# Output projection of a hybrid layer: eight units on features against seven half-size products on tokens

## The chip, the cores and the metric

The kernel runs on one core of one Trainium2 chip. The metric is the device time of one execution in microseconds (us), lower is better. Five engines of the core matter here, each with its own in-order queue: TensorE (PE, with its weight load PEld), VectorE (DVE), ScalarE (ACT), GpSimd (POOL), and SyncE (SP), which only issues transfers. DMAs are issued from the SP, ACT and POOL queues. A queue whose first instruction waits holds everything behind it.

## The reference, cut to what matters

One layer, D = 1024, S = 512 tokens, d_ff = 2816, float32 throughout:

```
u      = RMSNorm(x) * g1
z      = u @ w_in
A, B   = MoBA attention(z), chunkwise mLSTM(z)
merged = sigmoid(z_gA) * (A @ w_proj_a) + sigmoid(z_gB) * (B @ w_proj_b)
h      = x + merged @ w_out              # w_out is 1024 x 1024: the output projection
u      = RMSNorm(h) * g2
g, up  = split(u @ w_gate_up)
h      = h + (silu(g) * up) @ w_down
out    = RMSNorm(h) * g3
```

The change is in the line of `w_out` and in what leads from it into `w_gate_up`.

## The kernel before, in words

**Precision.** A float32 product is computed as three matmuls: an operand is split into a high part (rounded by an ACT copy, L148) and a low part (a DVE subtraction, L161), and high·high, low·high and high·low are accumulated in PSUM (`mm3`, L199 to L203). Every weight block therefore costs one ACT and one DVE instruction beside its matmuls.

**Up to the output projection.** Activations stand with features on the partitions and the 512 tokens along the free axis. `UNITS` lists 60 blocks of weights of 128x1024 in the order of their use: q, k, va, ob, vb, qkb, then `ga` and `gb` (gates, units 28 to 43), `p` (the two branch projections, 44 to 51) and `wo` (52 to 59). SP loads them in that order, 512 KB each, into seven buffers (`load_pair`, L186); `split_unit` makes high and low parts two units ahead. A unit is 24 matmuls of 128x512. `run_p` multiplies the projections by the sigmoid gates (L595 to L597) and splits the merged activations into `mgh` and `mgl`.

**The output projection before.** `run_wo(m)` gives 128 output features for all 512 tokens: 24 matmuls, DVE adds the residual (`xr`, L663), the ACT squares the sum (`add_sq`, with a running sum on DVE, L265), and the block is scaled by the second norm's gain (L669, L670, L678, L679). `residual()` transposes the previous block's sum to tokens (L647, four transposes), and stores it in DRAM as `h1d`, to which the down projection later adds.

**The feed-forward part.** Each of 22 `gu` items is a gate-and-up block computed as seven products of half size instead of eight (a Winograd form of Strassen's scheme): the activations are four quarters (two halves of the features by the two halves `A_` and `B_` of the tokens) and their sums, the seven operands `bq` being numbered 0 to 6; the weights are W11, W12, W22 and the sums S1 to S4, each product 12 matmuls of 128x256. `gu_load` loads the weights; the sum of two blocks (`s13`) is formed on the way in, by a POOL transfer that adds to what it finds (L705). S2 and S4 are formed by two DVE additions (L751, L752). The down projection (`ds`) uses the same scheme on tokens and adds its results to `h1d` by POOL transfers (L921).

**What sets the order.** A scheduler takes instructions by a priority. For the feed-forward part `plan()` gives each product a nominal start, and `at(key, w, off)` sets the priority of what follows to that start plus an offset. The queues keep that order at run time whatever the real times are. In the mLSTM, four loads of `R` from DRAM (L1377) stand on POOL's queue; L1389 is the first DVE instruction to use each.

Of the kernel before, what the change touches and what calls it, by code (L numbers as in the profile page):

```python
# [15 lines left out]
P = 128  # L16
# [31 lines left out]
WO = (0, 4, 1, 5, 2, 6, 3, 7)  # L48
# [36 lines left out]
def hybrid_layer_kernel(ctx: ExitStack, tc, xT, wall, wgu, wds, wdl, g3v, vecs, wgates, consts, rope, out):  # L85
# [103 lines left out]
    def split_unit():  # L189
# [3 lines left out]
        if u % 2 == 1:  # L193
            load_pair() if u < NGEN - 4 else st["load"]()

    def mm3(ps, wh, wl, wk, rh, rl, start, stop):

        n = len(wk)
        for j, k in enumerate(wk):  # L199
# [3 lines left out]
            T.matmul(ps, wh[:, c], rl[j], start=False, stop=stop and j == n - 1)  # L203
# [184 lines left out]
    def proj(wh, wl):  # L388
        ps = mmb()
        mm3(ps, wh, wl, range(8), uh, ul, True, True)  # L390
# [194 lines left out]
    def run_p(m, wh, wl):  # L585
        if m >= 6:
            load_xr()
        pa, pb = mmb(), mmb()
        mm3(pa, wh, wl, range(4), [t[0] for t in ya], [t[1] for t in ya], True, True)
        mm3(pb, wh, wl, range(4, 8), [t[0] for t in yb], [t[1] for t in yb], True, True)  # L590
# [6 lines left out]
        V.tensor_tensor(ga, ga, gb, op=ALU.add)  # L597
        mgd.append(split_hl(ga, "mg"))
# [4 lines left out]
    xr = []  # L603
    h1d = dram.tile([4, P, D], F32, name="h1d")
    ng2 = cst.tile([P, KT], F32, name="ng2")

    def load_xr():
        m = WO[len(xr)]
        t = act.tile([P, S], F32, name=nm("xr"), tag="X", bufs=NX)
        nc.sync.dma_start(t, xT[m])  # L610
        xr.append(t)

    bq = {}
    ut = {}  # L620
    HS = S // 2

    def bop(o, k):

        if o < 6:
            t = bq[(o // 2, k // 2)].rearrange("p x c -> p (x c)")
            b = 1024 * (k % 2) + HS * (o % 2)
            return t[:, b : b + HS], t[:, b + 512 : b + 512 + HS]
        t = bq[(3, 0)][:, k, :]
        return t[:, 0:HS], t[:, HS:S]  # L630

    def bpair(q, k):
# [6 lines left out]
    trq = []

    def residual():

        while trq:
            m, h = trq.pop(0)
            ps = sb()
            for t in range(4):
                T.transpose(ps[:, t * P : (t + 1) * P], h[:, t * P : (t + 1) * P], ident)  # L647
            o = slot(name="ht")
            act_(o, ps, AF.Copy)
            nc.scalar.dma_start(  # L650
                h1d[:, :, m * P : (m + 1) * P].rearrange("t p c -> p t c"), o.rearrange("p (t c) -> p t c", t=4)
            )

    def run_wo(i, wh, wl):
        if len(xr) < KT:
            load_xr()
        ps = mmb()
        mm3(ps, wh, wl, range(8), [t[0] for t in mgd], [t[1] for t in mgd], True, True)
        residual()
        yield  # L660
        m = i
        h = xr[WO.index(m)]
        V.tensor_tensor(h, ps, h, op=ALU.add)  # L663
        trq.append((m, h))
        a, b = h[:, 0:HS], h[:, HS:S]
        g, ng = col(G2 + m), ng2[:, m : m + 1]
        if m < 4:
            u = ut[m] = slot(name="ut")
            V.tensor_scalar(u[:, 0:HS], a, g, None, op0=ALU.mult)  # L669
            V.scalar_tensor_tensor(u[:, HS:S], b, ng, u[:, 0:HS], op0=ALU.mult, op1=ALU.add)  # L670
            hh, ll = bpair(0, m)
            act_(hh, u, AF.Copy, scale=-1.0)
            V.scalar_tensor_tensor(ll, u, -1.0, f(hh), op0=ALU.mult, op1=ALU.subtract)
        else:
            k = m - 4
            u = ut.pop(k)
            v = slot(name="v1")
            V.tensor_scalar(v[:, 0:HS], a, g, None, op0=ALU.mult)  # L678
            V.tensor_scalar(v[:, HS:S], b, ng, None, op0=ALU.mult)  # L679
            split_hl(v, dst=bpair(1, k))  # L680
            w = slot(name="v2")
            V.tensor_tensor(w[:, 0:HS], u[:, HS:S], v[:, HS:S], op=ALU.subtract)
            V.tensor_tensor(w[:, HS:S], u[:, 0:HS], w[:, 0:HS], op=ALU.subtract)
            split_hl(w, dst=bpair(2, k))
            V.tensor_tensor(u[:, 0:HS], v[:, 0:HS], w[:, 0:HS], op=ALU.subtract)
            if k == 0:
                bq[(3, 0)] = slot4(F32R, "bq")
            split_hl(u[:, 0:HS], dst=bop(6, k))
        add_sq(2, h, WO.index(m))

    run["wo"] = run_wo


# [5 lines left out]

    def gu_load(i):  # L700
# [3 lines left out]
        nc.sync.dma_start(s13, wgu[i][:, None, 0:512].to_broadcast([P, 2, 512]))  # L704
        nc.gpsimd.dma_start(s13, wgu[i][:, 512:1536].rearrange("p (x c) -> p x c", x=2), accum_op=ALU.add)  # L705
# [8 lines left out]
    def plan():  # L714
# [19 lines left out]
    def gu_prep(i):  # L734
        key = ("gu", i)
        g = sw[key]
        r, s13, w11 = g["r"], g["s13"], g["w11"]

        def hl(w, src, dst):
            at(key, w, -H_OFF)  # L740
            act_(dst[0], src, AF.Copy)
            at(key, w, -L_OFF)
# [46 lines left out]
    def prod(ps, w, o, first=False):  # L789

        wh, wl = w
        for k in range(4):
# [4 lines left out]
            T.matmul(ps, wh[:, c], bl, start=False, stop=k == 3, skip_group_check=not first)  # L797

    A_, B_ = slice(0, HS), slice(HS, S)

    def gu_first(i):
# [4 lines left out]
        prod(g["X"], g["W11"], 0, first=True)  # L806
# [4 lines left out]
    def gu_main(i):  # L811

        key = ("gu", i)
        g = sw[key]
        x, s12 = g["X"], g["s"]
        at(key, "S2")
        prod(x, g["S2"], 4)
        at(key, "S2", R_OFF)
        act_(s12[:, B_], x, AF.Copy)
# [9 lines left out]
        if i == 0:
            residual()  # L830
            rb2 = st["rb2"] = rstd_rows([ssum[2]])

            rc, nrc = st["rc"], st["nrc"] = [cst.tile([P, 4], F32, name=n_) for n_ in ("rc2", "nrc2")]
            columns(rb2[0:1, :], rc.rearrange("p (j h) -> p j h", h=1))
# [808 lines left out]
```

## Time and the profile before

| | |
|---|---|
| median of 3 runs | 733.4 us (733.3 to 733.64) |
| span of the profiled execution, first to last instruction | 731.3 us |
| PE busy | 721.8 us (99%) |
| DVE busy | 619.3 us (85%) |
| ACT busy | 431.4 us (59%) |
| POOL busy | 65.6 us (9%) |
| chain of work that ended last | PE 98% |
| granted TensorE clock, mean | 0.998 |

The page gives the profiled execution no time of its own beside the span; the span is 2.1 us below the median of the runs. Busy time of PE is modelled from matmul starts, and consecutive matmuls overlap in the rows, so the time that one takes on the path is the distance between the starts, not its duration. Times inside the trace are counted from the span's start. The output projection runs from about 349 to 399 us.

### The profile page before, as it was taken

The page shows a single profiled execution, that of the slowest core. Times are in us where ns is not written, and L with a number is a line of the kernel's source. Part 1 is how long each engine was busy: PE and PEld are TensorE (multiplying, and loading weights), DVE is VectorE, ACT ScalarE, POOL GpSimd, SP SyncE. Part 2 cuts the span into 40 slices and gives each one's busy share as a digit, 9 for nine tenths or more (in the row PEclk, how much of TensorE's full clock was granted, in tenths as well). Part 3 has the DMA queues.
Part 4 walks back from the last instruction along what each step waited for, and adds up shares of the span by engine and source line. Part 5 has one row for each costly group of instructions (what it writes and reads, how often), then busy time and mean ns, then how long its engine had stood idle before and what let it go on. Part 6 is the DMA issues. An engine that isn't in the chain of part 4 may idle for free.

```text
span 731.3 us, 11389 instructions
## 1 busy us (share of the span) xinstructions
PE 721.8 (99%) x4191; PEld 636.5 (87%) x4191; DVE 619.3 (85%) x1104; ACT 431.4 (59%) x747; POOL 65.6 (9%) x88
## 2 busy tenths in 40 slices
PE   9999999999999999999999999999999999999995
PEld 6888888888888888888888998999899899899984
DVE  6898877899987669566788999899899899989996
ACT  7535776668846339523456656665655565655555
POOL 0004010000000000000000000400310310130000
PEclk9999999999999999999999999999999999999999
DMA  8778573232431222534767353975995795596403
GB/s 315 273 226 226 185 215 110 80 125 94 164 136 58 87 86 88 173 106 124 185 177 203 128 160 93 240 216 128 210 266 146 167 276 166 146 249 200 151 0 117
DMA packets 51320, 118.74 MB, mean 162 GB/s; under 512 B 5292, under 2 KB 10292, under 8 KB 51264
## 3 DMA queue, kind: packets, MB, share of 16 engines
q1 hardware_dynamic: 37024, 88.95, 35.9%
q0 software_dynamic: 9728, 26.80, 19.2%
q10 hardware_dynamic: 4512, 2.26, 1.1%
q8 instruction: 33, 0.54, 0.3%
q14 instruction: 23, 0.19, 0.1%
HBM read 101.17 MB, written 16.82 MB: 161 GB/s over the span
## 4 chain that ended last, share of the span: by engine, by line
PE 98%; DMA 0%; ACT 0%; issue 0%; DVE 0%; SPq 0%; ACTq 0%
PE mm L201 13%; PE mm L203 12%; PE mm L202 12%; PE mm L795 6%; PE mm L796 6%; PE mm L797 6%; PE s L795 3%; PE s L797 3%; PE s L796 3%; PE mm L904 3%; PE mm L905 2%; PE mm L906 2%; PE mm L291 2%; PE acc L1358 2%; PE mm L479 2%; PE mm L480 2%
## 5 line engine op out<-in xcount | busy, mean ns | idle before, releaser
L148 ACT ACTIVATE wh<-raw 128x1024 fp32r<-128x1024 f32 x58 | 61.2, 1058 | 78.7 <-PE mm L202 75.7
L161 DVE TENSOR_TENSOR wl<-raw,wh 128x1024 fp32r<-128x1024 f32 x58 | 70.4, 1219 | 7.3 <-ACT wh L148 6.4
L795 PE MATMUL mm<-bq,w 128*128 128x256 f32 x264 | 75.5, 286 | 0.0
L796 PE MATMUL mm<-bq,w 128*128 128x256 f32 x264 | 74.9, 284 | 0.0
L797 PE MATMUL mm<-bq,w 128*128 128x256 f32 x264 | 74.8, 283 | 0.0
L743 DVE TENSOR_TENSOR w<-s,w 128x1024 fp32r<-128x1024 f32 x44 | 53.6, 1218 | 8.3 <-ACT w L148 8.1
L148 ACT ACTIVATE w<-s 128x1024 fp32r<-128x1024 f32 x44 | 46.5, 1056 | 14.5 <-PE mm L202 5.4
L201 PE MATMUL mm<-u,wh 128*128 128x512 f32 x136 | 53.6, 394 | 0.0
L202 PE MATMUL mm<-u,wl 128*128 128x512 f32 x136 | 53.2, 391 | 0.0
L203 PE MATMUL mm<-u,wh 128*128 128x512 f32 x136 | 53.1, 390 | 0.0
L203 PE MATMUL mm<-ul,wh 128*128 128x512 f32 x136 | 52.9, 389 | 0.0
L202 PE MATMUL mm<-uh,wl 128*128 128x512 f32 x136 | 52.9, 389 | 0.0
L201 PE MATMUL mm<-uh,wh 128*128 128x512 f32 x136 | 52.9, 389 | 0.0
L705 POOL DMA_DIRECT2D s<-in_wgu_dram x22 | 19.0, 862 | 368.0 <-DVE ga L597 132.0
L795 PEld LDWEIGHTS mm<-bq,w 128*128 128x128 f32 x264 | 50.6, 192 | 0.7 <-ACT s L148 0.3
L796 PEld LDWEIGHTS mm<-bq,w 128*128 128x128 f32 x264 | 50.6, 192 | 0.3 <-issue 0.2
L797 PEld LDWEIGHTS mm<-bq,w 128*128 128x128 f32 x264 | 50.6, 192 | 0.1
L148 ACT ACTIVATE w<-raw 128x1024 fp32r<-128x1024 f32 (+2 forms) x44 | 43.7, 995 | 11.7 <-PE s L796 3.3
L797 PE MATMUL s<-bq,w 128*128 128x256 f32 x176 | 49.8, 283 | 0.0
L796 PE MATMUL s<-bq,w 128*128 128x256 f32 x176 | 49.8, 283 | 0.0
L795 PE MATMUL s<-bq,w 128*128 128x256 f32 x176 | 49.8, 284 | 0.0
L148 ACT ACTIVATE w<-sw 128x1024 fp32r<-128x1024 f32 x20 | 21.2, 1060 | 22.4 <-DVE sw L782 20.3
(399 smaller groups left out, 2219.0 us busy)
## 6 DMA issues: line engine op xcount, KB each, us to landing
raw<-in_wall_dram SPq DMA_DIRECT2D x58, 512.0 KB, 3.6
s<-in_wgu_dram SPq DMA_DIRECT2D x22, 512.0 KB, 4.7
s<-in_wgu_dram POOLq DMA_DIRECT2D x22, 512.0 KB, 5.9
raw<-in_wgu_dram SPq DMA_DIRECT2D x22, 512.0 KB, 4.9
raw<-in_wds_dram SPq DMA_DIRECT2D x20, 512.0 KB, 5.9
w<-in_wgu_dram SPq DMA_DIRECT2D x22, 256.0 KB, 6.4
h1d<-s POOLq DMA_DIRECT2D x16, 256.0 KB, 8.8
R<-scr POOLq DMA_DIRECT2D x4, 896.0 KB, 4.6
```

The lines of the kernel that those rows point to most:

```text
L148: return A.activation(out_, in_, func, **kw)
L161: V.tensor_tensor(l, src, f(h), op=ALU.subtract)
L201: T.matmul(ps, wh[:, c], rh[j], start=start and j == 0, stop=False)
L202: T.matmul(ps, wl[:, c], rh[j], start=False, stop=False)
L203: T.matmul(ps, wh[:, c], rl[j], start=False, stop=stop and j == n - 1)
L291: T.matmul(ps01[j], w[:, j * P : (j + 1) * P], r, start=k == 0 and n == 0, stop=k == KT - 1 and n == 2)
L705: nc.gpsimd.dma_start(s13, wgu[i][:, 512:1536].rearrange("p (x c) -> p x c", x=2), accum_op=ALU.add)
L743: V.tensor_tensor(dst[1], src, f(dst[0]), op=ALU.subtract)
L795: T.matmul(ps, wh[:, c], bh, start=first and k == 0, stop=False, skip_group_check=not first)
L796: T.matmul(ps, wl[:, c], bh, start=False, stop=False, skip_group_check=not first)
L797: T.matmul(ps, wh[:, c], bl, start=False, stop=k == 3, skip_group_check=not first)
L904: T.matmul(ps, bh, wh[:, d], start=first and k == 0, stop=False, skip_group_check=not first)
```

## The change

**What it does.** The eight `wo` units are replaced by the seven-product scheme, with the four quarters of the merged activations (feature halves by token halves) as the stationary operand and the blocks of `w_out`, 512 columns wide, as the moving one: seven products (W11, W12, S1, S2, S4, S3, W22) of two token tiles of 12 matmuls each. The results stand on tokens.

- *Activations.* `run_p` writes the merged block into `mT`; `quarters_lo`, `quarters_a` and `quarters_b` form the seven operands `mq` with DVE sums and a high and a low part each.
- *Weights' sums.* S1, S2, S3 and S4 of `w_out` (`ws`), the sums `s13` of the first three `gu` items (`gs`) and S2, S4 of item 2 (`gt24`) are formed in DRAM: a copy on SP's queue (`wo_copy`), then an adding transfer on POOL's queue (`wo_sum`), placed by `SUMS` behind units 18 to 41 in issue order only (`behind` adds an order between instructions, no wait on the chip).
- *Residual.* Result tiles `ht[t, j]` are 128 tokens by 512 features. For the four tiles that a product writes first, ACT copies the PSUM bank and a POOL transfer adds `x` to the copy (L961); for the other four SP loads `x` (L973). All further products are added or subtracted by DVE (L965).
- *Back to features.* `to_features` (L935) transposes each tile, 32 transposes in all; ACT squares tiles with a summed output, stores them to `h1d`, and evicts the transposed blocks with the gain. `norm2` makes the norm from the four columns of sums on 128x4 tiles, and spreads it with one `ones` matmul in place of `rstd_rows` and its way through DRAM.
- *Order.* A table `Q` of offsets sets the priorities. The first products of `gu` items 0 and 1 are interleaved.

The diff, cut to its core:

```diff
-    u += [("wo", m) for m in WO]
+SUMS = {
+    18: [(1, "S1", (1, 0))], 20: [(0, "S1", (1, 1))], 22: [(1, "S2", "S1"), (1, "S3", (0, 0))],
+    24: [(0, "S2", (0, 0))], 27: [(1, "S4", "S2")], 29: [(0, "S4", (0, 1))], 31: [(0, "S3", (1, 0))],
+    33: [(1, 0, None), (1, 1, None)], 35: [(0, 0, None)], 36: [(0, 1, None), (1, 2, None)], 37: [(0, 2, None)],
+    38: [(1, i, "g") for i in G24], 39: [(0, i, "g") for i in G24], 41: [(0, i, "w") for i in G24],
+}
...
+            if u in SUMS:
+                with behind("unit"):
+                    for job, k, src in SUMS[u]:
+                        (wo_copy if job else wo_sum)(k, src)
...
-        mgd.append(split_hl(ga, "mg"))
+        V.tensor_tensor(mT[m // 4][:, m % 4, :], ga, gb, op=ALU.add)
+        if m == 3:
+            quarters_lo(mq, mT[0], slice(0, 4))
...
+    def wo_copy(k, src):
...
+        for e in range(2):
+            nc.sync.dma_start(ws[k][e], ws[src][e] if src in ws else wwo[src][e])
+
+    def wo_sum(k, src):
...
+        for e in range(2):
+            nc.gpsimd.dma_start(ws[k][e], wwo[src][e], accum_op=ALU.add, max_dma_last_dim=1024)
...
     def gu_load(i):
...
-        nc.sync.dma_start(s13, wgu[i][:, None, 0:512].to_broadcast([P, 2, 512]))
-        nc.gpsimd.dma_start(s13, wgu[i][:, 512:1536].rearrange("p (x c) -> p x c", x=2), accum_op=ALU.add)
+        if i < NGS:
+            nc.sync.dma_start(s13, gs[i])
...
+    def wo_prod(ps, w, o, t, first=False):
+        c = slice(t * P, (t + 1) * P)
+        for k in range(4):
+            h, l = w[k]
+            bh, bl = (x[:, 0, c] for x in bview(mq, o, slice(k, k + 1)))
+            T.matmul(ps, bh, h, start=first and k == 0, stop=False, skip_group_check=not first)
+            T.matmul(ps, bh, l, start=False, stop=False, skip_group_check=not first)
+            i = T.matmul(ps, bl, h, start=False, stop=k == 3, skip_group_check=not first)
...
+                marks[k, t] = wo_prod(bank[t], w[k], o, t, first=first)
+                at(WO_ITEM, k, U * (t + 1) + Q["add" + k])
+                if (t_ + t, j) not in ht:
+                    h = ht[t_ + t, j] = slot(name="ht")
+                    i = act_(h, bank[t], AF.Copy, scale=1.0 if op == ALU.add else -1.0)
+                    at(WO_ITEM, k, U * (t + 1) + Q["x"])
+                    marks["x"] = raw_ins(
+                        nc.gpsimd.dma_start(h, xtm[t_ + t][:, j * S : (j + 1) * S], accum_op=ALU.add)
+                    )
+                else:
+                    h = ht[t_ + t, j]
+                    i = V.tensor_tensor(h, h, bank[t], op=op)
...
+        stage("W11", 0, X, 0, 0, ALU.subtract, first=True)
...
+        stage("W12", 2, Y, 0, 0, ALU.add, first=True)
...
+        to_features("S1", Q["t00"], 0, 0)
+        stage("S1", 1, Z, 2, 1, ALU.add, first=True)
...
+        stage("S2", 4, X, 2, 0, ALU.subtract)
...
+        stage("S4", 3, Z, 2, 0, ALU.subtract)
+        to_features("S3", Q["t10"], 1, 0)
...
+        stage("S3", 5, X, 2, 1, ALU.add)
...
+        last_ = stage("W22", 6, X, 0, 1, ALU.add)
```

**PE, the start of the output projection.** Before, a unit's weight block (`wh`, `wl`) is the stationary operand and the merged activations (`mgh`, `mgl`) the moving one, and 24 matmuls into one bank `mm` stand between two groups of transposes; the rows are the end of the second unit.

```order
L201 MATMUL mm_3455<-mgh_3356,wh_3360 128x512
L202 MATMUL mm_3455<-mgh_3356,wl_3361 128x512
L203 MATMUL mm_3455<-mgl_3357,wh_3360 128x512
L201 MATMUL mm_3455<-mgh_3401,wh_3360 128x512
L202 MATMUL mm_3455<-mgh_3401,wl_3361 128x512
L203 MATMUL mm_3455<-mgl_3402,wh_3360 128x512
L647 MATMUL s_3480<-con,xr_3323 128x128 x4
```

After, on the same engine, 12 matmuls of the same size form one token tile of a product (the bank is `mm` or `acc`, the stationary quarter `bq`, the moving weights `w`); these rows are the end of the product W11 and the start of W12.

```order
L916 MATMUL mm_3492<-w_3347,bq_3253 128x512
L914 MATMUL mm_3492<-w_3347,bq_3253 128x512
L915 MATMUL mm_3492<-w_3348,bq_3253 128x512
L916 MATMUL mm_3492<-w_3347,bq_3253 128x512
L914 MATMUL acc_3518<-w_3351,bq_3457 128x512
L915 MATMUL acc_3518<-w_3352,bq_3457 128x512
L916 MATMUL acc_3518<-w_3351,bq_3457 128x512
```

The 192 matmuls of eight units became 168 of seven products, all of 128x512.

**DVE, around the first use of a tile with `x` added.** Before, DVE at the projection's first blocks reads PSUM and `xr` that SP loaded long ago (L663).

```order
L663 TENSOR_TENSOR xr_3323<-mm_3411,xr_3323 128x512
L669 TENSOR_SCALAR ut_3437<-xr_3323,vec 128x256
L161 TENSOR_TENSOR wl_3557<-raw_3366,wh_3556 128x1024
L670 SCALAR_TENSOR_TENSOR ut_3437<-xr_3323,ng_274,ut_3437 128x256
L673 SCALAR_TENSOR_TENSOR bq_3440<-ut_3437,bq_3440 128x512
L663 TENSOR_TENSOR xr_3368<-mm_3455,xr_3368 128x512
```

After, the first row below adds the product W12 to `ht_3489`, the tile that ACT wrote and POOL's transfer added `x` to; behind it in DVE's queue stand low parts of operands (L648) and of weights (L764).

```order
L965 TENSOR_TENSOR ht_3489<-ht_3489,acc_3518 128x512
L648 TENSOR_TENSOR bq_3468<-mT_3112,bq_3468 128x1024
L764 TENSOR_TENSOR w_3547<-raw_3508,w_3546 128x1024
L965 TENSOR_TENSOR ht_3505<-ht_3505,acc_3532 128x512
L764 TENSOR_TENSOR w_3551<-raw_3510,w_3550 128x1024
L648 TENSOR_TENSOR bq_3472<-mT_3112,bq_3472 128x1024
L764 TENSOR_TENSOR w_3617<-raw_3554,w_3616 128x1024
L764 TENSOR_TENSOR w_3621<-raw_3556,w_3620 128x1024
L764 TENSOR_TENSOR w_3695<-raw_3624,w_3694 128x1024
L965 TENSOR_TENSOR ht_3558<-ht_3558,mm_3476 128x512
```

A DVE instruction that needs a transfer's landing now stands ahead of nine others; nine rows behind the last one shown stands the addition of S4's product to the same `ht_3558`, which PE's transposes at the start of S3 read.

**POOL, from the loads of `R` to the output projection.** Before, the four loads of `R` are followed by the additions to the `gu` items' weights (`s`).

```order
L1377 DMA R_1764<-scr 128x1792
L1377 DMA R_2047<-scr 128x1792
L1377 DMA R_2124<-scr 128x1792
L1377 DMA R_2287<-scr 128x1792
L705 DMA s_3562<-in_wgu_dram 128x1024
L705 DMA s_3674<-in_wgu_dram 128x1024
```

After, sums of the weights in DRAM (`ws`, 512 KB each) stand before and between them, and the additions of `x` (`ht`) follow.

```order
L728 DMA ws_276<-in_wwo_dram 512x256
L728 DMA ws_277<-in_wwo_dram 512x256
L1662 DMA R_2145<-scr 128x1792
L728 DMA ws_278<-in_wwo_dram 512x256
L728 DMA ws_279<-in_wwo_dram 512x256
L1662 DMA R_2310<-scr 128x1792
L728 DMA ws_280<-in_wwo_dram 512x256
L728 DMA ws_281<-in_wwo_dram 512x256
```

The last load of `R` moved behind six adding transfers, the nearest two (`ws_278`, `ws_279`, the sum S4) directly ahead of it.

More of the change, by code (lines that the diff above doesn't have):

```diff
@@ L202, in mm3 @@
             T.matmul(ps, wl[:, c], rh[j], start=False, stop=False)
-            T.matmul(ps, wh[:, c], rl[j], start=False, stop=stop and j == n - 1)
+            i = T.matmul(ps, wh[:, c], rl[j], start=False, stop=stop and j == n - 1)
+        return raw_ins(i)
     man = ExitStack()
@@ L389, in proj @@
         ps = mmb()
-        mm3(ps, wh, wl, range(8), uh, ul, True, True)
+        marks["unit"] = mm3(ps, wh, wl, range(8), uh, ul, True, True)
         return ps
@@ L639, in hybrid_layer_kernel @@
[L639 to L659, printed above, removed]
-        yield
[L661 to L689, printed above, removed]
@@ L691, in hybrid_layer_kernel, with bview @@
-    run["wo"] = run_wo
+    ht = {}
+    mT = []
+    mq, bq = {}, {}
+    def bview(ops, o, k):
+        if o not in ops:
+            ops[o] = slot4(F32R, "bq")
+        t = ops[o].rearrange("p a c -> p (a c)")
+        n = HS * (k.stop - k.start)
+        return [t[:, 1024 * e + HS * k.start : 1024 * e + HS * k.stop].rearrange("p (k c) -> p k c", c=HS) for e in range(2)]
+    def bop(o, k):
+        t = bq[o].rearrange("p a c -> p (a c)")
+        return t[:, HS * k : HS * k + HS], t[:, 1024 + HS * k : 1024 + HS * k + HS]
@@ new lines, in hybrid_layer_kernel, with behind @@
+    marks = {}
+    @contextmanager
+    def behind(*keys):
+        traced = nc.cur_bb.bb.instructions
+        last = traced[-1]
+        yield
+        start = next(k for k in reversed(range(len(traced))) if traced[k] is last) + 1
+        for i in traced[start:]:
+            for key in keys:
+                m = marks[key]
+                tc.add_manual_dep(
+                    i, m.name,
+                    mybir.DependencyInfo(mybir.DependencyClass.NoSync, mybir.DependencyReason.DATA),
+                    reason="behind",
+                )
@@ L700, in gu_load @@
+    gs = [dram.tile([P, 2, S], F32, name=nm("gs")) for _ in range(NGS)]
     def gu_load(i):
@@ L796, in prod @@
             T.matmul(ps, wl[:, c], bh, start=False, stop=False, skip_group_check=not first)
[L797 to L799 removed]
+            i = T.matmul(ps, wh[:, c], bl, start=False, stop=k == 3, skip_group_check=not first)
+        return raw_ins(i)
+    def wo_prod(ps, w, o, t, first=False):
[6 more added lines that the diff above has]
+            i = T.matmul(ps, bl, h, start=False, stop=k == 3, skip_group_check=not first)
+        return raw_ins(i)
@@ new lines, in norm2 @@
+    def norm2():
+        at(ITEMS[0], "W11", Q["n2"])
+        v, q = cst.tile([P, 4], F32, name="v2"), cst.tile([P, 4], F32, name="q2")
+        s_ = ssq["t"]
+        V.scalar_tensor_tensor(v, s_[:, 0, :], EPS, s_[:, 1, :], op0=ALU.add, op1=ALU.add)
+        act_(q, v, AF.Ln)
+        act_(q, q, AF.Exp, scale=-0.5)
+        n_ = iter(range(9))
+        rc = st["rc"] = newton(q, v, lambda: cst.tile([P, 4], F32, name=f"rc2_{next(n_)}"))
+        nrc = st["nrc"] = cst.tile([P, 4], F32, name="nrc2")
+        V.tensor_scalar(nrc, rc, -1.0, None, op0=ALU.mult)
+        dg = slot(name="dg")
+        for t in range(4):
+            V.tensor_scalar(dg[:, t * P : (t + 1) * P], ident, rc[:, t : t + 1], None, op0=ALU.mult)
+        at(ITEMS[0], "W11", Q["n2b"])
+        ps = accb()
+        with tc.issue_after(marks["norm"]):
+            T.matmul(ps, ones, dg, start=True, stop=True)
+        rb2 = st["rb2"] = slot(name="rb2")
+        act_(rb2, ps, AF.Copy)
@@ L828, in gu_main @@
         prod(y, g["W12"], 2, first=True)
[L829 to L834, printed above, removed]
-            V.tensor_scalar(nrc, rc, -1.0, None, op0=ALU.mult)
         at(key, "W22", U_OFF)
```

352 lines of the change are left out of this document (292 added, 60 removed).

## The prediction

> **What bounds the kernel now.** I read the first lines of the page, then the waits of PE, then the windows of the stage that is changed, then the timelines of its engines.
>
> ```profile
> PE 721.8 (99%) x4191; PEld 636.5 (87%) x4191; DVE 619.3 (85%) x1104; ACT 431.4 (59%) x747; POOL 65.6 (9%) x88
> ...
> PE 98%; DMA 0%; ACT 0%; issue 0%; DVE 0%; SPq 0%; ACTq 0%
> ```
>
> ```profile
> core 0: 731.3 us, clock 0.998
> ```
>
> PE is the bound: the chain that ended last is PE for 98%, at a granted clock of 0.998. The table of what PE waited for in the whole trace has two rows:
>
> ```profile
> PE s L217 <- DVE zero L214: 1.2, 1, 1.2
> PE mm L291 <- ACT u L148: 0.5, 1, 0.5
> ```
>
> Both are at the start of the program (zeroed tiles and the first norm). From there to the last products nothing keeps PE waiting, so time goes in two ways only: fewer or smaller matmuls, or a new gap on PE. The windows are the last two branch-projection units and what leads to them (305 to 348.5), the output projection (348.5 to 392.6), the start of the feed-forward part, and the whole; the columns are busy time by engine with counts, the clock, and the DMA share.
>
> ```profile
> 305.00:348.50 43.50, 43.50 (x194) 36.03 (x193) 29.13 (x39) 13.84 (x17) 1.71 (x2) 1.00 0.36 112
> 348.50:392.60 44.10, 44.10 (x210) 36.48 (x209) 35.43 (x64) 22.57 (x35) 2.61 (x4) 1.00 0.74 188
> 305.00:420.00 115.00, 115.00 (x624) 99.32 (x623) 89.41 (x148) 55.66 (x83) 5.66 (x7) 1.00 0.54 153
> ```
>
> In 115 us DVE is busy for 89.4 and ACT for 55.7: DVE has 25.6 us free, which is not much, and it is in order, so a wait in the wrong place can pass to PE.
>
> **Term 1, the matmuls.** Thirteen consecutive starts inside a unit (first and last; a row is start, duration, instruction):
>
> ```profile
> 359.74 0.39 PE L203 MATMUL mm<-mgl,wh 128*128 128x512 f32 x1
> ...
> 362.46 0.39 PE L203 MATMUL mm<-mgl,wh 128*128 128x512 f32 x1
> ```
>
> Twelve steps in 2.72 us are 0.2267 us each; the duration 0.39 overlaps the next. Eight units of 24 are 192 matmuls; seven products of two tiles of 12 are 168, of the same 128x512 form. 24 x 0.2267 = 5.44 us fall off the path. That is the whole gain there can be: the transposes number 32 before and after, and the norm keeps one float32 `ones` matmul:
>
> ```profile
> 356.92 0.44 PE s L647 x4
> ...
> 398.78 0.44 PE s L647 x4
> 399.21 0.86 PE s L338 x2
> ```
>
> 0.11 us a transpose, 0.86 for the norm's, both unchanged. The runs' median stands 2.1 us above the span of the profiled execution (733.4 against 731.3), outside what is changed, so the same 2.1 is kept. With no new gap: 731.3 - 5.44 + 2.1 = 728.0.
>
> **Term 2, DVE and ACT work.** What is added, by duration:
>
> ```profile
> L663 DVE TENSOR_TENSOR xr<-mm,xr 128x512 f32<-128x512 f32 x8 | 5.5, 690 | 7.3 <-PE mm L203 7.3
> L161 DVE TENSOR_TENSOR wl<-raw,wh 128x1024 fp32r<-128x1024 f32 x4 | 4.9, 1217 | 0.0
> L265 DVE TENSOR_TENSOR sq<-sq,sq 128x512 f32<-128x512 f32 x6 | 4.1, 684 | 0.0
> ```
>
> Seven pairs of weight low parts of 128x1024 stand against eight (14 x 1.22 - 8 x 1.22 = +7.3). Seven low parts and four sums of 128x1024 replace eight low parts of 128x512 (11 x 1.22 - 8 x 0.69 = +7.9). Additions into result tiles are ten against eight (+1.4). Seven running sums of squares go (-4.8), and the two sums of `gu` item 2 (-1.4). That is about +10.4 us of DVE in a stretch with 25.6 free; by volume it is hidden. ACT gains some 6 high parts of 128x1024 and the copies, in 59 free. I cost both at nothing and look at order instead. Before the last projection units the work of PE is the same in the same order, and weights there are loaded a long way ahead.
>
> **Term 3, the residual on POOL's queue.** Take T = 0 at the first of the 168 matmuls. Distances between starts on DVE and ACT:
>
> ```profile
> 381.88 1.22 DVE L743 TENSOR_TENSOR w<-raw,w 128x1024 fp32r<-128x1024 f32 x1
> 383.02 0.42 DVE L682 TENSOR_TENSOR v<-ut,v 128x256 f32<-128x256 f32 x1
> 383.35 0.69 DVE L161 TENSOR_TENSOR bq<-v,bq 128x512 fp32r<-128x512 f32 x1
> 383.95 0.42 DVE L683 TENSOR_TENSOR v<-ut,v 128x256 f32<-128x256 f32 x1
> ```
>
> ```profile
> 380.39 1.06 ACT L148 ACTIVATE w<-raw 128x1024 fp32r<-128x1024 f32 x1 [1.78 <-PE mm L202]
> 381.36 0.58 ACT L148 ACTIVATE ht<-s 128x512 f32<-128x512 f32 x1
> ```
>
> So DVE takes 1.14 us for 1024 columns and 0.60 for 512 in a row, ACT 0.97 for 1024. The last branch projection ends at T = 0; three DVE rows at 0.60 finish the merged activations at about 2.0; ACT makes three high parts ahead of its copy of the first result tile, so that copy ends near 5.5 and the second, one more high part later, near 6.9. Then POOL's transfers add `x`. The first DVE row that waits for one (the first L965 in the order shown) stands ahead of the low parts for S2, S4, S3 and W22 and of all further additions. What an adding transfer costs in this trace:
>
> ```profile
> L705 POOL DMA_DIRECT2D s<-in_wgu_dram x22: 850/862/892, 336.9 to 656.8; - x22
> ...
> DMA to landing us min/median/max: 5.2/5.9/9.3
> ```
>
> ```profile
> raw<-in_wall_dram SPq DMA_DIRECT2D x58, 512.0 KB, 3.6
> ...
> h1d<-s POOLq DMA_DIRECT2D x16, 256.0 KB, 8.8
> ...
> xr<-in_xT_dram SPq DMA_DIRECT2D x8, 256.0 KB, 2.8
> ```
>
> L705 adds 512 KB into SBUF: 5.2 to 9.3, median 5.9. Additions of 256 KB into DRAM (`h1d`) take 8.8. The new one is 256 KB into SBUF; plain loads of 256 and 512 KB differ by 0.8, so I take 5.9 - 0.8 = 5.1, from L705, the nearest in kind, and keep both ends: 2.8 (a plain load of the same bytes) and 8.8.
>
> DVE resumes at 5.5 + 5.1 = 10.6. From that row to the addition of S4's product into the third tile are 19 rows, 7 of 1024 columns and 12 of 512: 7 x 1.14 + 12 x 0.60 = 15.2, so it is through at 25.8. PE gets there (120 matmuls and eight transposes, 120 x 0.2267 + 0.88) at 28.1. Four more rows (2.9) give the fourth tile at 28.7; PE wants it two transposes and seven matmuls later than the third, at 29.9. On paper that is 1.2 us to spare at the fourth tile; rows that depend on the one before cost more than 0.60 (I reckon 0.7), and with ten or so of these DVE comes out even with PE or a little behind: I estimate 0.5 us of gaps here, and 0.4 further on, where ACT squares tiles and DVE makes the operands of the first `gu` products behind the last additions. I put 0.9 in the sum. A later landing passes to PE almost whole: 1.8 with 5.9, 4.5 with 8.8; with 4.5 or less it is 0.2 or nothing. Who waits behind that row: low parts of operands and weights for the next products, so a late landing reaches PE once and is not made up, since PE has no slack to give.
>
> The Trainium skill, "DMA: Bandwidth & Descriptors", section "Anatomy of one DMA — SWDGE (gpsimd) path", gives 2.0 us plus bytes over 436 GB/s for a transfer of this queue. As an estimate from that page 256 KB would take 2.6 us, and the sum would be 728.0. The trace does not agree: the 512 KB that it would put at 3.2 took 5.9.
>
> **Term 4, sums in DRAM.** POOL and SP are otherwise nearly idle from 100 to 300 us, and the adding transfers of the `gu` items 0 to 2 leave the projection's stage (0.74 DMA share). The copies on SP's queue wait for POOL's sums, with weight loads behind them:
>
> ```profile
> L186 SPq DMA_DIRECT2D raw<-in_wall_dram x58: 327/328/430, 7.7 to 326.9; - x58
> L148 ACT ACTIVATE wh<-raw x58: 1044/1061/1067, 14.2 to 362.7; 128x1024 fp32r<-128x1024 f32 x58
> ```
>
> The last weight load is issued at 326.9 and first read by ACT at 362.7, 36 us later, so a copy that waits ten or twenty costs nothing. The one place with little in hand is the last load of `R`:
>
> ```profile
> 189.39 0.33 SPq L186 DMA_DIRECT2D raw<-in_wall_dram  x1
> ```
>
> ```profile
> 214.22 0.53 POOL L1377 DMA_DIRECT2D R<-scr  x1 [29.53 <-DVE wl L161]
> ```
>
> ```profile
> 219.94 1.14 DVE L1389 SCALAR_TENSOR_TENSOR R<-con,cS,R 128x128 f32<-128x128 f32 x4 [2.11 <-DMA R<-scr]
> 222.83 0.56 DVE L161 TENSOR_TENSOR Al<-R,Ah 128x384 fp32r<-128x384 f32 x1 [1.15 <-ACT Ah L148]
> ```
>
> ```profile
> 227.75 0.39 PE L1435 MATMUL acc<-Al,vb 128*128 128x512 f32 x1
> ```
>
> DVE already waits 2.11 us for it, and PE reads what DVE makes behind it (`Al`, done at 223.39) at 227.75, so a load that lands over 4.3 us later stops PE. The two 512 KB sums ahead of it cannot start before about 195 (their copies follow the weight load issued at 189.4), which leaves 19 us to 214.22. I cost this at nothing, bounded above by the rival below.
>
> **Sum.** 733.4 - 5.44 + 0.9 = 728.9, given as 729.0. The likeliest case by itself spans 728.0 to 730.0 (landings of 4.5 to about 6).
>
> **Rivals.** Two runs of this kernel differ from no change by what can be told only beyond about 0.2%, 1.5 us: faster is below 731.9, slower above 734.9.
>
> *The addition of `x` lands late.* If it behaves like the additions into DRAM, 8.8 to 9.3, DVE resumes at 14.4, and PE meets gaps of 4.5 at the third and fourth tile: 728.0 + 4.5 = 732.5, no change that can be told. For it: DMA share is high in the stage. Against it: the same instruction into SBUF had a median of 5.9 in windows with a share of 0.7 and more. One way to it would be that POOL's issue of a transfer is held up while DVE is busy. POOL's 22 issues of L705 took 850 to 892 ns although DVE was busy for 85%, which speaks against it; if it held for three times an issue, 2.6 more, a landing of 7.7 would give gaps of about 3.4 and 731.4; I give it 0.04 of the 0.20 below. The Trainium skill, "SBUF — State Buffer", section "SBUF: two separate sides", states such a rule as the trap in which descriptors cannot be written while DVE holds the shared port.
>
> *The other side: `R` late behind the sums.* If the two sums ahead of the last load of `R` run one after the other, each at the price of an addition into DRAM scaled by bytes (2 x 8.8 = 17.6), they end at 195 + 35 = 230, `R` lands at 235 instead of 219.9, 15 late, PE stops for 15 - 4.3 = 10.7, and the time is 728.0 + 10.7 = 738.7. It decides against the change (over 734.9) once the pair ends 6.9 + 4.3 = 11.2 us after 214.2. Against it: additions into DRAM in this trace overlap, six are issued within 7 us and still land after a median of 8.8:
>
> ```profile
> 457.36 2.10 POOL L921 DMA_DIRECT2D h1d<-s  x2
> 459.73 0.85 POOL L921 DMA_DIRECT2D h1d<-x  x1 [0.26 <-DVE x L955]
> ...
> 464.16 0.85 POOL L921 DMA_DIRECT2D h1d<-s  x1 [0.90 <-DVE s L961]
> ```
>
> *No gap at all*: 728.0, if the landing is near 4.5 or dependent rows cost nothing.
>
> **Numbers.** Forecast with gaps of up to 2 us: 0.48; no gap at all: 0.15. `x` late by either way, 730.0 to 733.2: 0.20, of which 0.08 below 731.9. `R` late or another long stop: 0.12, of which 0.01 stays below 734.9. The rest, 0.05, is small gains elsewhere in the new order, down to 727.3. Faster 0.48 + 0.15 + 0.08 + 0.05 = 0.76; same 0.12 + 0.01 = 0.13; slower 0.11. The range 727.3 to 732.9 leaves out the slow rival and the top of the late one.
>
> **What would show it.** Right: 168 L914 to L916 starts 0.227 apart; no wait of PE at the mLSTM; the transposes of the third and fourth tiles (L935) with waits for DVE L965 below 1 us in sum; DVE's first L965 waiting some 2 to 3 us for a DMA. The forecast is wrong if PE's waits for L965 sum to over 3 us, if DVE L1389 waits over 6 us for `R`, or if matmuls with float32r quarters as the stationary operand start further apart than 0.227.

## The result and the profile after

The changed kernel takes 727.8 us (727.7 to 728.38, four runs) against 733.39 for the kernel before: a ratio of 0.9925, 95% interval 0.9911 to 0.9939, 5.6 us faster. Its profiled execution has a span of 726.0 us against 731.3. The head of the page, its line on the chain that ended last, and the table of what PE waited for:

```profile
PE 716.9 (99%) x4167; PEld 632.5 (87%) x4167; DVE 623.5 (86%) x1094; ACT 441.9 (61%) x778; POOL 78.8 (11%) x100
...
PE 90%; DVE 3%; issue 2%; ACT 2%; DMA 1%; SPq 0%; POOLq 0%; ACTq 0%
```

```profile
PE s L230 <- DVE zero L227: 1.2, 1, 1.2
PE mm L304 <- ACT u L160: 0.2, 1, 0.2
PE mm L213 <- DVE ga L592: 0.2, 1, 0.2
```

PE has 24 matmuls fewer and 4.9 us less busy time, and none of its waits lies in the output projection. The chain's share fell from 98 to 90% without a matching wait: where a predecessor ends just as PE becomes free, the chain may step through it, so the share by itself says only that the margins are thin. The spacing is unchanged; thirteen starts of the new products (first and last) are again 2.72 us apart over twelve steps:

```profile
347.74 0.39 PE L915 MATMUL mm<-w,bq 128*128 128x512 f32 x1
...
350.46 0.39 PE L915 MATMUL mm<-w,bq 128*128 128x512 f32 x1
```

The windows (busy time by engine, clock, DMA share) show the price, paid beside PE: between 305 and 420 DVE is busy for 98.4 us where it was 89.4, ACT for 70.2 where it was 55.7, with PE still at 115.0 of 115.

```profile
305.00:346.80 41.80, 41.80 (x186) 34.62 (x185) 31.46 (x41) 15.06 (x18) 0.00 (x0) 1.00 0.50 165
346.80:391.00 44.20, 44.20 (x222) 37.26 (x221) 39.28 (x52) 32.84 (x62) 4.46 (x5) 1.00 0.70 203
...
305.00:420.00 115.00, 115.00 (x644) 100.40 (x643) 98.40 (x147) 70.16 (x119) 5.35 (x6) 1.00 0.57 175
```

The place on which the forecast turned is the wait for the residual. POOL's issue of the first addition of `x`, and the additions into result tiles on DVE (in the brackets what ended the wait ahead):

```profile
352.59 0.91 POOL L961 DMA_DIRECT2D ht<-in_xtm_dram  x1 [66.35 <-ACT ht L160]
```

```profile
356.97 0.69 DVE L965 TENSOR_TENSOR ht<-ht,acc 128x512 f32<-128x512 f32 x1 [1.56 <-DMA ht<-in_xtm_dram]
...
366.96 0.69 DVE L965 TENSOR_TENSOR ht<-ht,mm 128x512 f32<-128x512 f32 x1 [0.76 <-PE mm L916]
...
374.63 1.23 DVE L764 TENSOR_TENSOR w<-raw,w 128x1024 fp32r<-128x1024 f32 x1 [0.24 <-ACT w L160]
375.77 0.68 DVE L965 TENSOR_TENSOR ht<-ht,s 128x512 f32<-128x512 f32 x1
```

```profile
376.77 0.82 PE L935 MATMUL acc<-con,ht 128*128 128x128 f32 x6
```

The addition landed 4.3 us after its issue. DVE stood for 1.56 us, caught up, waited 0.76 for PE at the third tile and 0.24 for ACT behind it, and finished the fourth tile at 376.45; PE began to transpose it at 376.77. The stage holds with 0.3 us to spare there.

A last look at where the 5.3 us of span lie. The first matmul of the output projection starts later than before, not earlier. (Before, it starts at 345.87 and not at about 349, so the prediction's window from 348.5 leaves out its first dozen matmuls; no term of the sum uses that bound.)

```profile
345.87 0.39 PE L201 MATMUL mm<-mgh,wh 128*128 128x512 f32 x1
```

```profile
346.83 0.39 PE L914 MATMUL mm<-w,bq 128*128 128x512 f32 x1
```

0.96 us is lost ahead of the change: 0.6 at the start of the program, where the first unit of weights begins at 17.36 and not at 16.79 (in the other runs of the changed kernel and its variants at 16.8 to 17.4, so this differs from execution to execution), and most of the rest where the last load of `R` is used (below). From the first of these matmuls to the first store of the output (at 718.7 before, 713.8 after) 5.86 us are gained, 5.44 of it by the 24 matmuls; the other 0.4 is not explained. Another 0.35 of the span is gained behind that store.

### The profile page after: what moved, and what is told of

It reads as the page before. It is cut to its first block, busy times and chain, and to the rows that moved or that the text cites. A ratio compares the mean times of both kernels' runs of the same rounds, so it can differ in the third digit from the quotient of the medians.

```text
span 726.0 us, 11399 instructions
## 1 busy us (share of the span) xinstructions
PE 716.9 (99%) x4167; PEld 632.5 (87%) x4167; DVE 623.5 (86%) x1094; ACT 441.9 (61%) x778; POOL 78.8 (11%) x100
## 4 chain that ended last, share of the span: by engine, by line
PE 90%; DVE 3%; issue 2%; ACT 2%; DMA 1%; SPq 0%; POOLq 0%; ACTq 0%
PE mm L213 9%; PE mm L215 9%; PE mm L214 9%; PE mm L904 6%; PE mm L905 6%; PE mm L906 6%; PE s L904 3%; PE s L906 3%; PE s L905 3%; PE mm L1155 3%; PE mm L1156 3%; PE mm L1157 3%; PE mm L496 2%; PE mm L497 2%; PE mm L498 2%
## 5 line engine op out<-in xcount | busy, mean ns | idle before, releaser
L160 ACT ACTIVATE wh<-raw 128x1024 fp32r<-128x1024 f32 x50 | 52.8, 1057 | 62.2 <-PE mm L214 59.4
L160 ACT ACTIVATE w<-raw 128x1024 fp32r<-128x1024 f32 (+2 forms) x63 | 58.7, 944 | 24.1 <-PE mm L214 10.0
L173 DVE TENSOR_TENSOR wl<-raw,wh 128x1024 fp32r<-128x1024 f32 x50 | 60.7, 1220 | 7.5 <-ACT wh L160 6.6
L851 DVE TENSOR_TENSOR w<-s,w 128x1024 fp32r<-128x1024 f32 x42 | 51.2, 1219 | 7.1 <-ACT w L160 7.1
L160 ACT ACTIVATE w<-s 128x1024 fp32r<-128x1024 f32 (+1 forms) x46 | 46.7, 1020 | 8.4 <-DVE s L861 4.1
L777 POOL DMA_DIRECT2D s<-in_wgu_dram x19 | 16.7, 881 | 230.4 <-DVE acl L173 76.0
L160 ACT ACTIVATE s<-mm 128x256 f32<-128x256 f32 x44 | 16.6, 378 | 29.7 <-PE mm L906 29.7
```

The source lines that it names most:

```text
L160: return A.activation(out_, in_, func, **kw)
L173: V.tensor_tensor(l, src, f(h), op=ALU.subtract)
L851: V.tensor_tensor(dst[1], src, f(dst[0]), op=ALU.subtract)
```

## The experiments

Each was compared with the kernel before on the same chip, where that took 733.17 to 733.39 us; the times are set against 727.8, so differences of some 0.3 us say nothing.

**Only the matmuls: `before_168`.** In the kernel before, the projection's units without the last block of the contraction:

```diff
-        mm3(ps, wh, wl, range(8), [t[0] for t in mgd], [t[1] for t in mgd], True, True)
+        mm3(ps, wh, wl, range(7), [t[0] for t in mgd], [t[1] for t in mgd], True, True)
```

> The kernel before with each of its eight output-projection units cut from 24 to 21 matmuls (the last 128 of the contraction are left out), nothing else changed: 168 matmuls as in the changed kernel. Theory (the gain is the 24 matmuls at 0.2267 us): 733.4 - 5.44 = 728.0, within 0.5 of the changed kernel. Rival (the new order, the sums in DRAM or the interleaved gu products gain something by themselves, or DVE stops the shorter units): 1 us or more away from 727.8.

730.43 us (730.1 to 730.61), ratio 0.996 (0.9947 to 0.9972): 2.8 us faster than before, not 5.4. The new rows among PE's waits:

```profile
PE mm L795 <- DVE gt L842: 1.1, 1, 1.1
PE mm L795 <- ACT bq L148: 0.3, 1, 0.3
```

With the projection shorter, the first gate-and-up products catch up with DVE and ACT. Taking 24 matmuls out of an all-PE kernel is worth 5.4 us only if what runs beside them still fits; the old order had no room for it. Of the 2.6 us missing the two waits are 1.4, and counted from start to start 1.7, since a listed wait begins only at the modelled end of the matmul ahead, when the next could have started 0.16 us earlier. Some 0.7 more lies behind the last matmul, where the span ends 8.4 us later (7.7 in the changed kernel). The rest is not explained.

**The matmuls given back: `mm_192`.** The changed kernel with its first product done twice:

```diff
+                if k == "W11":
+                    wo_prod(bank[t], w[k], o, t, first=first)
                 marks[k, t] = wo_prod(bank[t], w[k], o, t, first=first)
```

> The changed kernel with the first product, W11, computed twice over the same banks (24 more matmuls of 128x512; the second pass starts the sums anew). Theory (PE is the bound everywhere, everything else of the change is hidden): 727.8 + 5.44 = 733.2. Rival (part of the new work on DVE and POOL stands on the path, which the added PE time would cover): less than 732.5.

732.77 us (732.58 to 733.0), ratio 0.9993 (0.9984 to 1.0001), no different from before. 24 matmuls cost 5.0 us, within 0.5 of their spacing, and of PE's waits the 1.2 us at the start alone remain. The missing 0.4 is the start of the program: the first unit begins at 16.98 here and at 17.36 in the changed kernel's profile. So the changed kernel's gain is the matmuls; all that was added beside them is covered.

**The interleaving undone: `no_interleave`.** The plan's sequence for the first two `gu` items:

```diff
-        seq = [(WO_ITEM, w) for w in WO_W] + [(i0, "W11"), (i0, "S1"), (i1, "W11"), (i1, "S1")]
-        seq += [(i, w) for i in (i0, i1) for w in ("S2", "S4", "S3")]
-        seq += [(i0, "W12"), (i0, "W22"), (i2, "W11"), (i1, "W12"), (i1, "W22")]
+        seq = [(WO_ITEM, w) for w in WO_W] + [(i0, "W11")]
+        for x, y in ((i0, i1), (i1, i2)):
+            seq += [(x, "S2"), (x, "S1"), (x, "W12"), (x, "S3"), (y, "W11"), (x, "S4"), (x, "W22")]
```

> The changed kernel with the first two gu items one after the other again (W11, S2, S1, W12, S3 of item 0, then W11 of item 1, S4, W22 of item 0, and so on, as before) in place of the interleaved order; all work kept. In the kernel before with 168 matmuls PE met 1.4 us of waits for DVE and ACT at the first gu products. Theory (the interleaving is what keeps PE busy while the last tiles pass through DVE and ACT): 1 to 4 us slower than 727.8, waits of PE at L905 to L907, more if one gap lasts over 3 us, since the granted clock then falls to 0.5. Rival (the interleaving is not needed): 727.8 within 0.6.

731.35 us (731.14 to 732.38), ratio 0.9974 (0.9966 to 0.9983): 3.5 us of the 5.6 are gone. PE's waits (lines are one higher here; L1038 is the norm's matmul):

```profile
PE acc L1038 <- DVE dg L1034: 1.5, 1, 1.5
...
PE s L905 <- ACT gt L160: 0.7, 1, 0.7
PE mm L905 <- ACT s L160: 0.4, 1, 0.4
```

The three waits are 2.6 us; counted from start to start they are 3.1 (1.7, 0.9 and 0.5), and a shift of 0.3 at 394.2 that is too short to be listed makes up nearly all of the 3.5. The interleaved items are the cover under which the last tiles and the norm pass through DVE and ACT. The offsets in `Q` stood unchanged, so a plan tuned for this order might lose less.

**The ties undone: `no_behind`.** `behind` ignores all keys but `"unit"`:

```diff
             for key in keys:
+                if key != "unit":
+                    continue
```

> The changed kernel without the ties of the weight splits to matmuls (the `behind` of W11, W12, S1 and p; the ties of the DRAM sums to their units are kept), so that the scheduler places the splits by priority alone. Theory (the ties only settle a place in DVE's and ACT's queues in which there is about 1 us to spare): between 727.5 and 730. Rival (they keep DVE's queue free of waits for late weights): over 730, with PE waits for L965 or low parts.

727.47 us (727.07 to 728.0), ratio 0.9922 (0.9908 to 0.9935), no different from the changed kernel. PE's waits are those of the start alone, and DVE waits 1.8 us for `x` where it waited 1.56. The ties of weight splits to matmuls carry nothing that a measurement can tell; the ties of the DRAM sums to units were left in place.

**The sums of the `gu` weights back in SBUF: `no_gs`.**

```diff
-NGS = 3
-G24 = (2,)
+NGS = 0
+G24 = ()
```

> The changed kernel with the sums of the first three gu items formed as before (POOL transfers adding into SBUF in the projection's stage, and item 2's S2 and S4 on DVE), the sums of w_out still in DRAM. Theory (DVE has room by volume, but POOL's additions of x then stand behind or beside 512 KB additions): 727.8 to 729. Rival (the sums in DRAM are what makes room): over 729, with a later landing of x or DVE waits for s13.

734.82 us (732.62 to 735.91), ratio 1.0015 (1.0005 to 1.0025): 7.0 us lost, and the change is worth nothing. One of the additions on POOL's queue again, ACT's wait for it, and PE's (lines are two lower here; L933 is the transposes):

```profile
367.23 1.35 POOL L775 DMA_DIRECT2D s<-in_wgu_dram  x1
```

```profile
381.98 1.06 ACT L158 ACTIVATE w<-s 128x1024 fp32r<-128x1024 f32 x1 [7.42 <-DMA s<-in_wgu_dram]
```

```profile
PE acc L933 <- ACT ut L158: 5.0, 1, 5.0
...
PE s L902 <- ACT gt L158: 1.1, 1, 1.1
```

This addition, issued at 367.23 right behind the second pair of additions of `x`, lands at 381.9, after 14.7 us; ACT's split of its tile waits 7.4 us at the head of ACT's queue, and behind it stand the evictions (`ut`) of the transposed tiles, whose PSUM banks PE needs. The two gaps are 6.1 us; some 1.5 more goes to the clock, which was 0.5 from 385.5 to 388.9. It is not the addition of `x` that suffers (DVE waits 1.3 us for it) but ACT, which the prediction had costed at nothing.

**Only item 2's sums back on DVE: `no_g24`.** `G24 = ()`, `gs` kept.

> The changed kernel with gs (s13 of items 0 to 2) still formed in DRAM, but S2 and S4 of item 2 formed by two DVE additions as before. Theory (the loss of 7 us without the sums in DRAM came from ACT waiting for the POOL addition of item 1's weights, so gs carries it): 727.8 within 0.7. Rival (the room on DVE carries it): over 729.

728.86 us (728.63 to 729.13), ratio 0.9941 (0.9928 to 0.9953): 1.1 us slower, more than expected, and a wait of the same size:

```profile
PE s L904 <- ACT gt L160: 1.1, 1, 1.1
```

The same wait of 1.1 us stands among PE's in `no_gs` (L902 there), so by difference some 6 of the 7 us belong to `gs` and 1 to `gt24`.

**The residual later: `x_pieces128`, `x_pieces64`, `x_first128`.** The same additions with smaller pieces (in the third only those of W11), the order of DVE, ACT, PE and SP untouched:

```diff
-                        nc.gpsimd.dma_start(h, xtm[t_ + t][:, j * S : (j + 1) * S], accum_op=ALU.add)
+                        nc.gpsimd.dma_start(h, xtm[t_ + t][:, j * S : (j + 1) * S], accum_op=ALU.add, max_dma_last_dim=128)
```

> The changed kernel with POOL's four additions of x cut into pieces of 128 bytes instead of 2 KB, the order of all engines the same, so that they land later; the landing L of the first (4.3 us in the changed kernel) is read from the trace. Theory (DVE's queue behind the first addition has about 1 us to spare, idle 0.76 us at the third tile's first addition): no change up to L of about 5.4, and from there 1 us on PE for each us: 727.8 + (L - 5.4). Rival 1, the prediction's sum: 1.8 at L = 5.9, 4.5 at 8.8. Rival 2: the wait is made up in the stage, 727.8 for L up to 9.

> As the run before with pieces of 64 bytes: a later landing still. Theory: 727.8 + (L - 5.4), with PE waiting for DVE's additions (L965) at the transposes of the third and fourth tile, or for operands behind them. Rival 2 (made up): 727.8.

> The changed kernel with only the first pair of POOL's additions of x in pieces of 128 bytes, the order of all engines the same. In the run with all four in pieces the first landed 6.0 us after its issue and PE waited 0.9 us at the fourth tile; the rest of its loss came from the second pair and the half clock behind that gap. Theory: a gap of about 0.9 and no loss of clock, 727.8 + 0.9 = 728.7. Rival, the prediction's price: 1.8 for a landing of 5.9, 729.6. Rival (the loss came from the first pair after all): over 731.

With all four in pieces of 128 bytes: 735.47 us (734.05 to 735.95), ratio 1.0026 (1.0016 to 1.0035). POOL, DVE and PE:

```profile
353.10 4.28 POOL L961 DMA_DIRECT2D ht<-in_xtm_dram  x2 [66.84 <-ACT ht L160]
```

```profile
359.19 0.69 DVE L965 TENSOR_TENSOR ht<-ht,acc 128x512 f32<-128x512 f32 x1 [3.71 <-DMA ht<-in_xtm_dram]
...
387.36 0.69 DVE L965 TENSOR_TENSOR ht<-ht,mm 128x512 f32<-128x512 f32 x1 [3.99 <-DMA ht<-in_xtm_dram]
```

```profile
377.95 0.87 PE L935 MATMUL acc<-con,ht 128*128 128x128 f32 x6 [0.87 <-DVE ht L965]
...
388.10 1.54 PE L935 MATMUL acc<-con,ht 128*128 128x128 f32 x6 [3.79 <-DVE ht L965]
...
389.87 0.63 PE L915 MATMUL mm<-w,bq 128*128 128x512 f32 x1
390.30 0.63 PE L916 MATMUL mm<-w,bq 128*128 128x512 f32 x1
```

The first addition lands after 6.0 us and costs a gap of 0.87. The second pair, for the two tiles to which S3's product is added, lands after 9.7 and 17.0 us and costs 3.79; and the matmuls behind that gap start 0.43 apart, not 0.227. The windows there show why, in the column of the clock:

```profile
388.00:390.00 2.00, 1.90 (x8) 1.80 (x9) 0.64 (x2) 1.26 (x4) 0.00 (x0) 0.50 1.03 215
390.00:392.00 2.00, 2.00 (x6) 1.52 (x5) 0.00 (x0) 1.55 (x4) 0.00 (x0) 0.50 0.34 113
392.00:396.00 4.00, 4.00 (x17) 3.27 (x16) 3.43 (x6) 2.87 (x6) 0.00 (x0) 0.79 0.06 25
```

Half the clock from 388 to about 393.7 is some 2.8 us lost on top: 0.87 + 3.79 + 2.8 = 7.5 of the 7.7 measured. With 64 bytes it is 747.44 us (746.3 to 750.21), ratio 1.019 (1.0176 to 1.0204), with 17.6 us of such waits, three in number. The longest of them, 8.0 us, comes already with the first pair, whose second addition POOL issued only 5.8 us after it was done with the first; the trace names no cause:

```profile
361.69 3.16 POOL L961 DMA_DIRECT2D ht<-in_xtm_dram  x1 [5.79 <-issue]
```

The formula put down for both, 1 us for each us of the first landing, left out the other additions and the clock. With the first pair alone in pieces the time is 728.53 us (728.3 to 728.88), ratio 0.9936 (0.9922 to 0.9949). DVE's first addition, PE's wait and its transposes are

```profile
359.01 0.69 DVE L965 TENSOR_TENSOR ht<-ht,acc 128x512 f32<-128x512 f32 x1 [3.71 <-DMA ht<-in_xtm_dram]
```

```profile
PE acc L935 <- DVE ht L965: 0.9, 1, 0.9
```

```profile
377.77 0.88 PE L935 MATMUL acc<-con,ht 128*128 128x128 f32 x6 [0.88 <-DVE ht L965]
```

The addition landed after 6.0 us; DVE's first row came 2.0 us later than in the changed kernel (359.01 for 356.97) and PE's transposes 1.0 later (377.77 for 376.77), at full clock. So about 1 us was to spare in the first pair's landing, as expected, and the price is half of what the prediction had given.

**The residual by SP: `x_sp`.** All eight tiles loaded by SP, POOL's additions gone:

```diff
+        at(WO_ITEM, "W11", -Q["x0"])
+        load_x(0, 0)
...
+        load_x(2, 1)
```

> The changed kernel with x of all eight tiles loaded by SP and added by DVE (four more DVE additions of 128x512, four ACT copies and the four POOL transfers fewer), the scheduler placing them anew. Theory (the addition on POOL is covered in the changed kernel, so taking it away gains nothing): 727.8 within 0.6, or slower by what four DVE rows of 0.6 us displace. Rival (the wait of 1.56 us of DVE for x costs PE something elsewhere): 727.0 or less.

729.69 us (729.12 to 730.78), ratio 0.9955 (0.9943 to 0.9968): 1.9 us slower. DVE does not wait for `x` any more, but PE waits once, before the first `gu` products:

```profile
394.52 0.39 PE L904 MATMUL mm<-bq,w 128*128 128x256 f32 x1 [2.02 <-ACT s L160]
```

```profile
396.00:398.00 2.00, 2.00 (x12) 2.00 (x12) 1.47 (x3) 1.71 (x4) 0.00 (x0) 0.51 0.09 28
398.00:400.00 2.00, 2.00 (x13) 2.00 (x13) 2.00 (x3) 1.94 (x2) 0.00 (x0) 0.64 0.28 103
```

The clock falls again, after a wait of 2.02 us. The profile is of the slowest of the five executions: two took 730.7 to 730.8 us, three 729.1 to 729.7. The fall costs the profiled one some 1.7 us (half of 3.4); the three are faster than it by 1.1 to 1.7, which fits the same gap without the fall, but is not shown. The addition on POOL is no burden to be removed: it takes four additions from DVE. Since the scheduler also placed other rows anew, it stays open how much of the 1.9 the four rows make.

**`R` later: `R_pieces256`.** The last load of `R` in pieces of 256 bytes, every engine's order the same:

```diff
-        nc.gpsimd.dma_start(t, scr[h : h + 1, :].partition_broadcast(P))
+        nc.gpsimd.dma_start(t, scr[h : h + 1, :].partition_broadcast(P), **(dict(max_dma_last_dim=256) if len(rbc) == 3 else dict()))
```

> The changed kernel with the last load of R cut into pieces of 256 bytes, the order of all engines the same, so that it lands later than the 6.0 us of the changed kernel. Prediction's rival: 4.3 us to spare before PE stops, so no change for up to 10 us of landing. Theory (the first consumer behind it on DVE is ga, L592, which frees the PSUM bank that PE needs 0.2 us later, as the wait of 0.2 us at L213 shows): each us of delay stops PE for one us, and beyond a gap of about 2 us half the clock for some us costs 2 to 3 more.

731.02 us (729.54 to 731.47), ratio 0.9968 (0.9957 to 0.9979): 3.2 us slower. In the kernel before, the rows behind the first use of `R` are these: DVE's `ga` ends at 221.67, and PE's next unit of weights starts at 221.73.

```profile
220.99 0.68 DVE L575 TENSOR_TENSOR ga<-mm,rn 128x512 f32<-128x512 f32 x1
```

```profile
221.73 0.50 PE L201 MATMUL mm<-u,wh 128*128 128x512 f32 x1
```

Now DVE's and PE's rows of the changed kernel, then of this one:

```profile
220.69 1.14 DVE L1674 SCALAR_TENSOR_TENSOR R<-con,cS,R 128x128 f32<-128x128 f32 x4 [2.40 <-DMA R<-scr]
```

```profile
222.48 0.50 PE L213 MATMUL mm<-u,wh 128*128 128x512 f32 x1 [0.21 <-DVE ga L592]
```

```profile
222.44 1.14 DVE L1674 SCALAR_TENSOR_TENSOR R<-con,cS,R 128x128 f32<-128x128 f32 x4 [4.54 <-DMA R<-scr]
```

```profile
224.23 0.50 PE L213 MATMUL mm<-u,wh 128*128 128x512 f32 x1 [2.34 <-DVE ga L592]
```

```profile
222.00:226.00 4.00, 1.77 (x6) 1.39 (x7) 3.56 (x8) 2.86 (x6) 0.00 (x0) 0.86 1.23 197
226.00:230.00 4.00, 4.00 (x14) 3.22 (x13) 0.84 (x2) 0.00 (x0) 0.00 (x0) 0.71 0.55 161
```

`R` lands after 8.1 us, not 6.0. DVE's wait grows by 2.14 us and PE's by 2.13: nothing is to spare. The rest is the clock: by the two windows it stood at 0.5 for some 3.4 us (4 x 0.14 / 0.5 and 4 x 0.29 / 0.5), and twelve steps behind the gap take 1.5 us more than at full clock. Together that is 3.6 us; this execution, 3.3 us longer than the changed kernel's, had begun its first unit 0.4 earlier. One of the six took 729.54 us, 1.4 less than any other, which fits the same gap without the fall of the clock.

## Why the prediction came out right, and which of its sizes were off

- **Term 1, the matmuls: right in size.** 5.44 us was expected and 24 matmuls measured 5.0 when given back. What it said in passing, that nothing but fewer matmuls or a gap can matter, is borne out; but `before_168` shows that the term is not the change's by right. Half of it comes only with the new order behind it.
- **Term 2, DVE and ACT by volume: right for the result, thin as an argument.** DVE grew by 9.0 us between 305 and 420 (10.4 was summed), ACT by 14.5, and PE was not stopped. Yet `no_gs`, `no_interleave` and `no_g24` lose 7.0, 3.5 and 1.1 us with volumes that would fit as well. Order decided, and for ACT the prediction had not looked at it beyond the copies of the first tiles.
- **Term 3, the residual: over-sized by 0.9, the whole difference between 729.0 and 727.8 but 0.3.** DVE's resumption, 10.1 us after the first matmul, was forecast for 10.6, the fourth tile at 29.6 for 28.7 plus the dependents, PE's need of it at 29.9 for 29.9. The landing was 4.3 against 5.1, and the 0.4 put down for places further on did not occur. That DVE comes out about even with PE was right partly by luck: in place of the dependents' extra time, DVE stood for 1.0 us on the way (0.76 for PE, 0.24 for ACT). These waits are what a later landing uses up first, so it does not pass to PE "almost whole". The price was too high near by (1.8 for 5.9; 0.9 in all was measured at 6.0) and too low far out, since it left out the other additions and the clock: 4.5 was given for 8.8, where `x_pieces64`, whose additions landed after 8.3 to 14.9, lost 19.6.
- **Term 4, `R`: the step that failed, without harm.** The margin of 4.3 us was read from PE's use of `Al`. Between `L1389` and `Al` stands `ga` (L575 before, L592 after), which frees a PSUM bank that PE needs sooner; the margin is nil, and was so before the change (0.06 us between the rows shown). The rival's threshold of 11.2 us was wrong by all of that, and by the clock. It did not come about because the sums had landed: POOL issued them at 201.90 and 203.10, 7 us later than the prediction had allowed, they landed by 211.9, and `R` was issued at 214.68. `R` came 0.8 us later on DVE than before, 0.6 of it the later start of the program, for 0.2 us of wait.
- **The rule on POOL's issue being held up by DVE** found no support: the four additions of `x` were issued in 872 to 1237 ns (the longest right behind another) with DVE busy for 89% of the stage.
- **What lies outside the terms** nearly cancels, and that is luck: 0.96 us was lost ahead of the projection, 0.4 and 0.35 gained behind its start and behind the first store without a known cause, and the median lies 1.8 us above the span, where the sum had kept 2.1.

## What to carry to other kernels

Where one engine is busy for 99%, fewer instructions on it pay their spacing times their number only if every queue beside it still arrives in time. Test the ceiling by leaving the instructions out of the old kernel (here 2.8 of 5.4 us), and look for the cover in the order of the next stage and in work that can be done stages earlier (here 3.5 and 7.0 us). Read the margin of a wait from the first instruction behind it that anybody needs, also one that only frees a bank, and not from the data's own path. Price a gap on PE of two microseconds or more at its length and often some 1.5 to 3 us more for the clock.

## What the runs showed of the hardware

The granted clock falls after short gaps on PE. After waits of 0.88, 1.54 and 1.78 us (`x_first128`, `no_interleave`, one of the three in `x_pieces64`) it stayed at 1.00; after 2.02 us (`x_sp`) it was about 0.5 for some 3.4 us, beginning 1.5 us after PE resumed, and after 2.34 us (`R_pieces256`) for 3.4 us, beginning 0.7 us after; after 3.79 us (`x_pieces128`) it was 0.5 from before the resumption on, for 5.6 us behind it.

The stretches at half rate last 3.4 us or about two or three times that; the column of the clock in `no_gs`, in `x_pieces128`, and behind the two gaps of 8 us in `x_pieces64`:

```profile
385.50:388.90 3.40, 2.98 (x8) 2.31 (x9) 3.37 (x6) 2.22 (x7) 0.87 (x1) 0.50 0.89 270
```

```profile
386.90:393.70 6.80, 5.60 (x16) 4.65 (x17) 2.75 (x5) 3.55 (x10) 0.00 (x0) 0.50 0.54 116
```

```profile
367.40:374.20 6.80, 3.16 (x11) 2.88 (x12) 3.91 (x4) 3.18 (x5) 0.00 (x0) 0.50 1.11 113
398.20:408.30 10.10, 5.88 (x17) 4.92 (x18) 3.04 (x5) 3.83 (x10) 0.00 (x0) 0.50 0.75 90
```

So they look like steps of about 3.4 us that do not begin with the gap or with its end. That would also explain why executions of one kernel fall in two groups 1.0 us and more apart (`x_sp`, `R_pieces256`); this was not tested.

The Trainium skill, "TensorE: Matmul & The Clock Gate", section "Why this matters for your kernels", asks for no idle gaps above about 3 us. The half rate agrees with these traces; the length does not, for a wait of 2.0 us was enough in the profiled execution here. Between 1.8 and 2.0 us no gap lies.

In the changed kernel the four POOL additions of 256 KB into SBUF landed after 4.3 to 9.4 us, the eight of 512 KB into DRAM (`ws`) after a median of 8.8. Cutting the additions of the first pair into pieces of 128 bytes raised POOL's issue of the two from 0.9 to about 2.1 us each and the first landing from 4.3 to 6.0.
